# Newton's rounds of 26 small reciprocal square roots moved from VectorE to GpSimd in a 1-core transformer kernel

## The chip, the core and the metric

The kernel runs on one core of a Trainium2 chip. The core has a TensorE (PE in the profile; its weight loads are shown apart as PEld), a VectorE (DVE), a ScalarE (ACT), a GpSimd (POOL), and a SyncE (SP) that issues most of the transfers. Each engine works through its own queue in order; semaphores tie the engines together. The metric is device time in microseconds, the median of several executions. Inputs and outputs are float32.

## What is computed

Two transformer blocks on 256 tokens of width 1024. The first has two attentions side by side (a: global with grouped keys, b: a mixture of dilated windows), each with 8 heads of 64, whose q and k are normed per head and whose outputs are normed over all 512 columns:

```python
qa = apply_axial_rope(rms_norm(qa, qa_norm_g), tables)
ka = apply_axial_rope(rms_norm(ka, ka_norm_g), tables)
out_a = global_gqa_attention(qa, ka, va)
out_b = dilated_mixture_attention(rms_norm(qb, qb_norm_g), rms_norm(kb, kb_norm_g), vb)
mixed = jnp.concatenate([rms_norm(out_a, outa_norm_g), rms_norm(out_b, outb_norm_g)], axis=-1)
x = x + mixed @ w_out
x = x + conv_ffn(rms_norm(x, norm2_g), w_up, conv_w, conv_b, w_down)
```

The second block has two layers, each on 256 latent and 256 context tokens: a differential attention of 8 heads, a Mamba-2 scan beside it, and an MLP. Each head's output is normed per token:

```python
a = p[:, 0] - lam * p[:, 1]
o = jnp.einsum('bhqk,bkhe->bqhe', a, v)
...
(rmsnorm(o, subln_g) * (1.0 - lam_init))
```

In layer 1, the last, only the latent tokens' queries are computed (`lat_only`).

## The kernel before

Matrix products run on TensorE as three fp32r products (high by high, low by high, high by low). ScalarE casts a weight's high part (`whi`, `whB`), VectorE computes the low part (`wlo` at L137, `wlB` at L211), a 128x1024 subtraction each. Weights stream in while products run.

A norm needs 1/sqrt(v), which `rsqrt` (L213) computes without a table: L218 shifts the bits of v, L220 subtracts them from a magic number, and three rounds of Newton's method follow, L223 to L225, in place on two small tiles `nwt` and `nwy`. All of it is on VectorE, 128 partitions by 2, 4 or 8 columns. `rsqrt` is called 26 times:

- In the first block 10 times: `rt` for the tokens' norm (its consumers are ScalarE's `vA`, `vB`), the kv tile and six q and k tiles in `hstat` (consumers L569, L539, L542, L544; behind them ptq, the transposes on TensorE), and once for each half of the output in `weigh` (`mra`, `mrb`): L642 scales `oa` or `ob`, and ptm transposes it for the output product.
- In each attention of the second block 8 times, once per head, in `headnorm`: L1205 and L1206 prepare v, `rsqrt` follows, L1209 writes the normed head `o` from the accumulator `po`, and in the next step `headout` has TensorE transpose it (pto; two or four 128x128).

The attention of the second block is a software pipeline over units of a head: scores of unit i (pss on TensorE, maxima L1163 and L1164 on VectorE, exponentials `pr` on ScalarE), the transposes ptp of unit i−1, the weighing po of unit i−2, and the head's norm when its last unit is weighed. Between these steps a background stream puts products of the following heads' q, k and v (psq, psk, psv), of gates (psgs) and, at the end, of the scan (psB, psC, psxs) on TensorE. While `self.pin` is set, the order of TensorE's instructions stays nearly as the program writes it; the order on the other engines is the scheduler's, which places each instruction by its own estimates. `dk` (L1032) is a tile of the scan's decays that VectorE writes within head 1 of layer 0, from TensorE's ptcs and psdec. GpSimd has little to do: some memsets at the start, seven sums of squares (L444), the zeroing of halves of `klo` (L1099) for each head, and sums of squares in the scan (L1570, L1573).

Of the kernel before, what the change touches and what calls it, by code (L numbers as in the profile page):

```python
# [25 lines left out]
ADD, SUB, MUL, MIN, MAX = ALU.add, ALU.subtract, ALU.mult, ALU.min, ALU.max  # L26
# [78 lines left out]
class Build:  # L105
# [107 lines left out]
    def rsqrt(self, v, pool, n, tag="nw"):  # L213
        nc = self.nc
        p = v.shape[0]
        ti = pool.tile([p, n], F32, tag=tag + "t", name="nwt")
        y = pool.tile([p, n], F32, tag=tag + "y", name="nwy")
        nc.vector.tensor_scalar(out=ti.bitcast(I32), in0=v.bitcast(I32), scalar1=1, scalar2=None,  # L218
                                op0=ALU.arith_shift_right)
        nc.vector.tensor_scalar(out=y.bitcast(I32), in0=ti.bitcast(I32), scalar1=-1.0,  # L220
                                scalar2=float(0x5F3759DF), op0=MUL, op1=ADD)
        for _ in range(3):
            nc.vector.tensor_tensor(out=ti, in0=y, in1=y, op=MUL)  # L223
            nc.vector.scalar_tensor_tensor(out=ti, in0=ti, scalar=-0.5, in1=v, op0=MUL, op1=MUL)
            nc.vector.scalar_tensor_tensor(out=y, in0=ti, scalar=1.5, in1=y, op0=ADD, op1=MUL)  # L225
        return y

    def fnorm(self, src, kts, n, dim, pool):
# [1794 lines left out]
```

## Time and profile before

| | |
|---|---|
| Time, median of 3 runs | 2373.35 us (2372.89 to 2373.66) |
| The profiled execution | 2373.57 us |
| Its span, first to last instruction | 2371.8 us |
| Mean granted clock of TensorE | 0.996 |
| Busy: PE / PEld / DVE / ACT / POOL | 98% / 86% / 73% / 57% / 2% |
| GpSimd | 57.7 us in 68 instructions |

Busy time is the union of an engine's spans; a matmul's end is modelled, so a busy TensorE may still wait within a span. An instruction of VectorE, ScalarE or GpSimd lengthens the kernel only where TensorE, or the chain that ends last, waits for it.

### The profile page before, as it was taken

Reading aid. Unit: us, or ns where it says so; the run is one execution under the profiler, and the core shown is the slowest. Engines: PE = TensorE matmul, PEld = TensorE weight load, DVE = VectorE, ACT = ScalarE, POOL = GpSimd, SP = SyncE. Lnnn points to the kernel's source line nnn. Section 1 sums busy time; section 2 is a strip of 40 time slices with the busy share of each in tenths; the row PEclk is TensorE's granted clock in tenths of the full one; section 3 lists DMA queues with packets and bytes.
Section 4 is the critical chain, followed back from the end, with each engine's and each line's share of the span. In section 5 each row is a group of like instructions: output and inputs, shape, how many; then the busy total and the mean of one; then the engine's idle time right before and its main releaser. Section 6 shows DMA issues by size and latency. Waiting matters only on the chain.

```text
span 2371.8 us, 39549 instructions
## 1 busy us (share of the span) xinstructions
PE 2317.3 (98%) x15566; PEld 2036.8 (86%) x15566; DVE 1738.7 (73%) x3466; ACT 1345.2 (57%) x2681; POOL 57.7 (2%) x68
## 2 busy tenths in 40 slices
PE   8999999999999999999999999999999999999998
PEld 7889998888887887778897877899898888899998
DVE  6678866777687878996474334388788999976776
ACT  5566546667565666764243233247776676655553
POOL 1000000000000000100000000000000000000000
PEclk9999999999999999999999999999999999999999
DMA  7557674112433343336343453353224444365553
GB/s 273 172 190 263 227 256 147 57 71 67 112 116 128 114 138 120 114 124 229 110 140 145 153 220 126 123 189 121 92 94 143 156 134 161 115 214 179 189 184 107
DMA packets 75034, 356.59 MB, mean 150 GB/s; under 512 B 9184, under 2 KB 16352, under 8 KB 38368
## 3 DMA queue, kind: packets, MB, share of 16 engines
q1 hardware_dynamic: 71088, 349.31, 42.5%
q10 hardware_dynamic: 3760, 4.75, 0.6%
q8 instruction: 122, 2.00, 0.3%
q14 instruction: 64, 0.52, 0.1%
HBM read 340.15 MB, written 13.89 MB: 149 GB/s over the span
## 4 chain that ended last, share of the span: by engine, by line
PE 84%; DVE 8%; ACT 6%; issue 1%; DMA 1%; POOL 0%; SPq 0%; DVEq 0%; ACTq 0%; POOLq 0%
PE psm L331 22%; PE psxs L331 6%; PE psso L331 6%; PE psu L331 5%; PE psz L331 4%; PE psk L331 3%; PE psao L331 3%; PE psga L331 3%; PE psd L331 3%; PE psB L331 3%; PE psgs L331 2%; PE pso L331 2%; PE psv L331 2%; PE psy L331 2%; PE psC L331 2%; PE po L331 2%
## 5 line engine op out<-in xcount | busy, mean ns | idle before, releaser
L136 ACT CAST whi<-raw 128x1024 fp32r<-128x1024 f32 (+1 forms) x430 | 445.2, 1043 | 530.6 <-PE psm L331 262.0
L137 DVE TENSOR_TENSOR wlo<-raw,whi 128x1024 fp32r<-128x1024 f32 (+1 forms) x430 | 521.8, 1218 | 213.6 <-ACT whi L136 209.1
L331 PE MATMUL psm<-dh,whi 128*128 128x256 f32 (+1 forms) x576 | 182.7, 317 | 0.5 <-DVE x L1784 0.5
L331 PE MATMUL psm<-dl,whi 128*128 128x256 f32 (+1 forms) x576 | 182.4, 317 | 0.0
L331 PE MATMUL psm<-dh,wlo 128*128 128x256 f32 (+1 forms) x576 | 182.3, 317 | 0.0
L331 PE MATMUL psm<-hhi,whi 128*128 128x258 f32 (+2 forms) x544 | 179.5, 330 | 1.7 <-ACT whi L136 1.2
L331 PE MATMUL psm<-hlo,whi 128*128 128x258 f32 (+2 forms) x544 | 179.1, 329 | 0.4 <-DVE hlo L920 0.3
L331 PE MATMUL psm<-hhi,wlo 128*128 128x258 f32 (+2 forms) x544 | 177.8, 327 | 0.5 <-DVE wlo L137 0.5
L1485 ACT ACTIVATE E<-R,cstok 128x128 f32<-128x128 f32 x384 | 120.0, 390 | 37.4 <-PE psy L331 28.3
L331 PEld LDWEIGHTS psm<-dh,whi 128*128 128x128 f32 x576 | 108.6, 189 | 9.3 <-issue 1.9
L331 PEld LDWEIGHTS psm<-hhi,whi 128*128 128x128 f32 x544 | 103.1, 190 | 15.1 <-issue 2.9
L331 PEld LDWEIGHTS psm<-dh,wlo 128*128 128x128 f32 x576 | 108.7, 189 | 7.5
L331 PEld LDWEIGHTS psm<-dl,whi 128*128 128x128 f32 x576 | 108.5, 188 | 7.4
L331 PE MATMUL psxs<-hhi,whi 128*128 128x512 f32 x256 | 113.0, 442 | 0.0
L1784 DVE SCALAR_TENSOR_TENSOR x<-psm,mod,x 128x256 f32<-128x256 f32 x96 | 44.1, 482 | 93.1 <-PE psm L331 93.1
L331 PEld LDWEIGHTS psm<-hlo,whi 128*128 128x128 f32 x544 | 103.2, 190 | 9.3 <-DVE hlo L920 1.2
L331 PEld LDWEIGHTS psm<-hhi,wlo 128*128 128x128 f32 x544 | 103.2, 190 | 9.2 <-DVE wlo L137 0.7
L331 PE MATMUL psxs<-hlo,whi 128*128 128x512 f32 x256 | 100.3, 392 | 0.0
L331 PE MATMUL psxs<-hhi,wlo 128*128 128x512 f32 x256 | 100.2, 392 | 0.0
L1346 DVE SCALAR_TENSOR_TENSOR xT<-psxs,halfw,xT 128x510 f32<-128x510 f32 (+1 forms) x128 | 94.6, 743 | 0.5 <-ACT xT L1342 0.2
L1166 ACT ACTIVATE pr<-pss,mx 128x512 f32<-128x512 f32 (+1 forms) x96 | 58.4, 614 | 61.4 <-DVE mx L1164 60.3
L331 PE MATMUL psu<-hhi,whi 128*128 128x256 f32 x320 | 91.6, 286 | 0.5 <-ACT hhi L800 0.5
(487 smaller groups left out, 7002.6 us busy)
## 6 DMA issues: line engine op xcount, KB each, us to landing
raw<-in_w_m SPq DMA_DIRECT2D x68, 1024.0 KB, 4.9
araw<-in_ada SPq DMA_DIRECT2D x48, 1024.0 KB, 5.2
R<-csd SPq DMA_DIRECT2D x48, 512.0 KB, 6.2
raw<-in_w_up SPq DMA_DIRECT2D x22, 1024.0 KB, 4.9
raw<-in_w_qk SPq DMA_DIRECT2D x16, 1024.0 KB, 4.9
raw<-in_w_bc SPq DMA_DIRECT2D x16, 1024.0 KB, 5.0
raw<-in_w_xs SPq DMA_DIRECT2D x16, 1024.0 KB, 4.9
raw<-in_w_z SPq DMA_DIRECT2D x16, 1024.0 KB, 5.0
```

The source lines that it names most:

```text
L136: nc.scalar.copy(h, r)
L137: nc.vector.tensor_tensor(out=lo[:, :nk, :n], in0=r, in1=h.bitcast(F32), op=SUB)
L331: i = self.nc.tensor.matmul(*args, **kw)
L1166: nc.scalar.activation(out=pt_[:, i * kw:(i + 1) * kw], in_=ps[:, i * kw:(i + 1) * kw], func=AF.Exp, scale=0.125, bias=mx[:, i:i + 1], acc ...
L1346: nc.vector.scalar_tensor_tensor(out=y[:, :, lo:hi], in0=u[:, :, lo + o:hi + o], scalar=wj(j), in1=y[:, :, lo:hi], op0=MUL, op1=ADD)
L1485: nc.scalar.activation(out=E[:, d, h, :], in_=R[:, d, h, :], func=AF.Relu, scale=-1.0, bias=self.cs_tok[:, c, i:i + 1])
L1784: nc.vector.scalar_tensor_tensor(out=xs[col][:, k, :], in0=ps[:, t], scalar=self.mod[l][:, 40 + k, col:col + 1], in1=xs[col][:, k, :], op0 ...
```

## The change

The two integer steps of `rsqrt` stay on VectorE. Each round of Newton's method becomes four GpSimd instructions in place of three on VectorE: VectorE's fused form (multiply by a scalar, then by a tensor) is taken apart. All 26 calls change; the rounds' arithmetic is the same but for the order of roundings. Behind L222 the line numbers of the changed kernel are two higher.

```diff
--- before.py
+++ after.py
@@ -219,10 +219,12 @@
                                 op0=ALU.arith_shift_right)
         nc.vector.tensor_scalar(out=y.bitcast(I32), in0=ti.bitcast(I32), scalar1=-1.0,
                                 scalar2=float(0x5F3759DF), op0=MUL, op1=ADD)
+
         for _ in range(3):
-            nc.vector.tensor_tensor(out=ti, in0=y, in1=y, op=MUL)
-            nc.vector.scalar_tensor_tensor(out=ti, in0=ti, scalar=-0.5, in1=v, op0=MUL, op1=MUL)
-            nc.vector.scalar_tensor_tensor(out=y, in0=ti, scalar=1.5, in1=y, op0=ADD, op1=MUL)
+            nc.gpsimd.tensor_tensor(out=ti, in0=y, in1=y, op=MUL)
+            nc.gpsimd.tensor_tensor(out=ti, in0=ti, in1=v, op=MUL)
+            nc.gpsimd.tensor_scalar(out=ti, in0=ti, scalar1=-0.5, scalar2=1.5, op0=MUL, op1=ADD)
+            nc.gpsimd.tensor_tensor(out=y, in0=ti, in1=y, op=MUL)
         return y
 
     def fnorm(self, src, kts, n, dim, pool):
```

GpSimd's queue now holds the rounds in the order of the calls, with the memsets between them. Before, the queue holds nothing of them; the rows below stand at head 0 of layer 0 (ss is v, nwt and nwy the two small tiles).

```order
L1101 MEMSET klo 64x512 x6
L224 TENSOR_TENSOR nwt<-nwy 128x4
L225 TENSOR_TENSOR nwt<-nwt,ss 128x4
L226 TENSOR_SCALAR nwt<-nwt 128x4
L227 TENSOR_TENSOR nwy<-nwt,nwy 128x4
L224 TENSOR_TENSOR nwt<-nwy 128x4
```

Two more rounds and two memsets of klo follow, and then head 1's rounds; a round waits for the one before it, and the first for VectorE's L220.

On VectorE at the same place, before (rt, rot and qhl belong to the q product of a later head, mx to the maxima of a next unit, o to this head):

```order
L220 TENSOR_SCALAR nwy<-nwt 128x4
L1070 TENSOR_TENSOR rot<-rot,cons 128x256
L223 TENSOR_TENSOR nwt<-nwy 128x4
L1111 TENSOR_TENSOR qhl<-psq_5160,qhl 64x256
L224 SCALAR_TENSOR_TENSOR nwt<-nwt,ss 128x4
L1071 TENSOR_TENSOR rot<-rt,rot 128x256
...
L1163 TENSOR_REDUCE mx_5311<-pss_5309 128x2
L224 SCALAR_TENSOR_TENSOR nwt<-nwt,ss 128x4
L1164 TENSOR_SCALAR mx_5300<-mx_5300 128x2
L1164 TENSOR_SCALAR mx_5311<-mx_5311 128x2
L225 SCALAR_TENSOR_TENSOR nwy<-nwt,nwy 128x4
L1209 TENSOR_TENSOR o_5238<-po_4806,nwy 128x512
```

And now:

```order
L220 TENSOR_SCALAR nwy<-nwt 128x4
L1072 TENSOR_TENSOR rot<-rot,cons 128x256
L1113 TENSOR_TENSOR qhl<-psq_5190,qhl 64x256
L1073 TENSOR_TENSOR rot<-rt,rot 128x256
L1113 TENSOR_TENSOR qhl<-psq_5190,qhl 64x256
L1211 TENSOR_TENSOR o_5271<-po_4836,nwy 128x512
L1113 TENSOR_TENSOR qhl<-rot,qhl 64x256 x2
L1165 TENSOR_REDUCE mx_5333<-pss_5331 128x2
L1165 TENSOR_REDUCE mx_5344<-pss_5342 128x2
```

Before, the nine instructions of the rounds took turns with ten others; now L1211 (L1209 of before) stands five rows behind L220, and two of the qhl rows and the maxima have moved behind it. At the other heads L1211 stands right behind L220, or with one wlo, wlB or maximum between.

On TensorE, most rows are where they were; at the last two heads of each layer pto has moved. At head 6 of layer 0, before (psB are products of the scan in the background, pto the transposes of the head's o, ptp those of a unit's probabilities):

```order
L331 MATMUL psB<-hhi,wlo 128x512
L331 MATMUL psB<-hhi,whi 128x512
L331 MATMUL psB<-hlo,whi 128x512
L331 MATMUL psB<-hhi,wlo 128x512
L331 MATMUL psB<-hhi,whi 128x512
L326 MATMUL pto_7122<-cons,o_7063 128x128 x4
L331 MATMUL po_6933<-V,pT_7079 128x128 x4
L326 MATMUL ptp_7135<-cons,pr_7006 128x128 x4
L331 MATMUL psB<-hlo,whi 128x512
```

And now:

```order
L333 MATMUL psgs<-hhi,wlo 128x512
L333 MATMUL psB<-hhi,whi 128x512
L333 MATMUL psB<-hlo,whi 128x512
L328 MATMUL pto_7173<-cons,o_7114 128x128 x4
L333 MATMUL po_6981<-V,pT_7130 128x128 x4
L328 MATMUL ptp_7186<-cons,pr_7054 128x128 x4
L333 MATMUL psB<-hhi,wlo 128x512
L333 MATMUL psB<-hhi,whi 128x512
L333 MATMUL psB<-hlo,whi 128x512
```

Of the seven psB matmuls that stood between the gate's and pto, two still do, and five come behind ptp. At head 7 of layer 0 pto has moved ahead by one matmul, at head 6 of layer 1 by four.

## Rows read from the trace of the kernel before

**Rows 1.** The page: span, and part 1, busy time (share) xinstructions.

```profile
span 2371.8 us, 39549 instructions
...
PE 2317.3 (98%) x15566; PEld 2036.8 (86%) x15566; DVE 1738.7 (73%) x3466; ACT 1345.2 (57%) x2681; POOL 57.7 (2%) x68
```

**Rows 2.** TensorE's waits: who for whom, us in total, times, longest.

```profile
PE pto L326 <- DVE o L1209: 9.4, 5, 3.4
...
PE pto L326 <- DVE dk L1032: 2.2, 1, 2.2
PE ptm L326 <- DVE oa L642: 2.0, 2, 1.7
```

**Rows 3.** Timeline of TensorE: start, us, instruction, [idle time before, releaser].

```profile
448.40 0.66 PE L326 MATMUL pto<-cons,o 128*128 128x128 f32 x4 [3.44 <-DVE o L1209]
...
535.82 0.60 PE L326 MATMUL pto<-cons,o 128*128 128x128 f32 x4
...
613.58 0.39 PE L331 MATMUL psB<-hhi,wlo 128*128 128x512 f32 x1
613.81 0.39 PE L331 MATMUL psB<-hhi,whi 128*128 128x512 f32 x1
614.10 0.66 PE L326 MATMUL pto<-cons,o 128*128 128x128 f32 x4
...
627.73 0.66 PE L326 MATMUL pto<-cons,o 128*128 128x128 f32 x4 [0.27 <-DVE o L1209]
...
1672.73 0.69 PE L326 MATMUL pto<-cons,o 128*128 128x128 f32 x2 [3.19 <-DVE o L1209]
...
1801.76 0.41 PE L326 MATMUL pto<-cons,o 128*128 128x128 f32 x2 [0.34 <-DVE o L1209]
```

**Rows 4.** Stretches: busy us of each engine, granted clock (PEclk), DMA, GB/s.

```profile
core 0: us, PE busy (x) PEld busy (x) DVE busy (x) ACT busy (x) POOL busy (x), PEclk, DMA share, GB/s
449.80:453.30 3.50, 3.50 (x11) 2.73 (x10) 3.46 (x8) 2.79 (x5) 0.00 (x0) 0.51 0.00 0
478.80:485.00 6.20, 3.97 (x27) 3.46 (x26) 4.46 (x14) 2.90 (x10) 0.00 (x0) 1.00 0.00 0
1671.80:1678.60 6.80, 5.87 (x28) 5.87 (x29) 5.21 (x16) 6.02 (x16) 0.00 (x0) 0.50 0.44 153
```

**Rows 5.** Tile nwt: xcount, ns min/median/max, first and last start, shapes.

```profile
L223 DVE TENSOR_TENSOR nwt<-nwy x78: 152/161/171, 20.5 to 1800.6; 128x2 f32<-128x2 f32 x33, 128x4 f32<-128x4 f32 x27, 128x8 f32<-128x8 f32 x18
```

**Rows 6.** Timeline of VectorE.

```profile
16.01 1.36 DVE L211 TENSOR_TENSOR wlB<-raw,whB 128x1024 fp32r<-128x1024 f32 x1 [1.14 <-ACT whB L210]
...
442.38 0.16 DVE L220 TENSOR_SCALAR nwy<-nwt 128x4 int32<-128x4 int32 x1
...
447.65 0.69 DVE L1209 TENSOR_TENSOR o<-po,nwy 128x512 f32<-128x512 f32 x1
...
533.72 0.69 DVE L1209 TENSOR_TENSOR o<-po,nwy 128x512 f32<-128x512 f32 x1
...
610.41 0.17 DVE L220 TENSOR_SCALAR nwy<-nwt 128x4 int32<-128x4 int32 x1
...
1667.28 0.17 DVE L220 TENSOR_SCALAR nwy<-nwt 128x2 int32<-128x2 int32 x1
...
1799.22 0.17 DVE L220 TENSOR_SCALAR nwy<-nwt 128x2 int32<-128x2 int32 x1
...
1801.18 0.42 DVE L1209 TENSOR_TENSOR o<-po,nwy 128x256 f32<-128x256 f32 x1
```

**Rows 7.** Timeline of GpSimd.

```profile
0.24 0.10 POOL L2014 MEMSET const-float32-0.0<- 128x1 f32 x1 [0.24 <-issue]
...
16.43 2.32 POOL L444 TENSOR_TENSOR sqa<-sqa,sq 128x256 f32<-128x256 f32 x2 [0.15 <-ACT sq L443]
```

**Rows 8.** Tile sqa on GpSimd: xcount, ns min/median/max.

```profile
L444 POOL TENSOR_TENSOR sqa<-sqa,sq x7: 724/742/1520, 12.2 to 18.0; 128x256 f32<-128x256 f32 x7
```

**Rows 9.** Tile ssq on GpSimd.

```profile
L1573 POOL TENSOR_TENSOR ssq<-ssq,u x19: 1288/1615/1934, 710.0 to 2089.1; 128x512 f32<-128x512 f32 x19
```

## The prediction, before the changed kernel was run

> **What bounds the kernel now.** I first read the busy shares: TensorE (PE) is at 98% and VectorE (DVE) at 73%, while GpSimd (POOL) works 57.7 us of 2371.8 [rows 1]. So a VectorE instruction costs time only where TensorE stands waiting for it. Next comes the table of TensorE's waits. Its longest entry is the one that this change touches: pto, the transposes of a head's normed output o, waited 9.4 us for o in five places. ptm, the transposes of the first block's output, waited 2.0 us for oa, and one pto waited 2.2 us for dk [rows 2]. The table has six waits of pto in all, for sixteen heads, so at ten heads TensorE arrived no earlier than its data. Where it did wait, the rows give the price: 3.44 us at the first head of layer 0, 3.19 us at the first of layer 1, 0.27 and 0.34 us at the last head of each layer [rows 3]; at ptm it was 1.7 [rows 2].
>
> After the two long gaps the granted clock is 0.51 in 449.80 to 453.30 and 0.50 in 1671.80 to 1678.60, the lower of TensorE's two levels (1.2 GHz, not 2.4) [rows 4]. TensorE was busy for 3.50 and 5.87 us there; at the full clock this would be half, so these stretches cost about 1.7 and 2.9 us on top of the gaps.
>
> **What the change takes from VectorE.** A call of rsqrt loses nine VectorE instructions; 26 calls lose 234, at 161 ns each 37.7 us of busy time [rows 5]. I cost this gain at nothing by itself, since VectorE is not the bound. It counts in the chain from L220 to the consumer: in the last head of layer 1, where nothing is interleaved, L220 starts at 1799.22 and takes 0.17, and L1209 starts at 1801.18. That is 1.79 us for nine instructions [rows 6].
>
> **What it adds on GpSimd.** Twelve instructions in a row, each needing the one before. The trace has no GpSimd arithmetic on 2 to 8 columns, so I bound it. Below: the smallest GpSimd instruction is a 128x1 memset of 0.10 us [rows 7]. Above: the 128x256 TENSOR_TENSOR, 0.74 us at the median and 0.72 at the least [rows 8]. The 128x512 one takes 1.29 at the least [rows 9], so 256 columns more cost 0.56 us, 2.2 ns each, and the line through both has about 0.16 us left at no columns. Between dependent instructions there is a gap: the pair at 16.43 took 2.32 us, and 1.52 (the longest) and 0.72 of it are work, so 0.08 is gap [rows 7, 8]. I take 0.16 + 0.08 = 0.24 us for one, an estimate, since 2 to 8 columns are nearest to the line's end at none; 12 of them are 2.88 us. A handover to GpSimd showed 0.15 us of idle time after ScalarE's release [rows 7]; with two of about 0.14, to and from VectorE, the chain is 3.16 us in place of 1.79. **An exposed call loses 1.4 us.** At the lower bound (0.18 per instruction, 2.44 in all) it loses 0.65; at the upper bound (0.82, 10.1 in all) 8.3. With 0.35 it loses 2.7.
>
> **The order changes too.** VectorE's remaining instructions used to be slipped between the rounds; now L1209 stands almost directly behind L220, and the max reductions come after it. Of the first heads this matters most.
> - Layer 0, head 0: L220 starts at 442.38 and L1209 at 447.65, 5.3 us for a chain that needs 1.8 by itself, because ten others stand between [rows 6]. Then L220 ends at 442.54, L1209 could start at 445.70, take 0.69, and pto follow 0.06 later, at 446.45 in place of 448.40 [rows 3]: **−1.9**.
> - Layer 1, head 0: L220 ends at 1667.45 [rows 6], so by the same sum pto could run at 1671.1 in place of 1672.73, −1.6. But one 1.22 us wlB stands between. The row of L211 that met GpSimd's 128x256 took 1.36 us while that one took 1.52 in place of 0.74 [rows 6 to 8]: the two hold each other up. With wlB's whole length added the gain is −0.4. I take **−1.0**.
>
> The page "SBUF — State Buffer" of the Trainium skill, section "SBUF: two separate sides", states that a VectorE instruction with two SBUF inputs and a GpSimd one that reads SBUF take the shared port pair by an exclusive lock, for the whole instruction. The row of 1.52 us agrees; by it the gain at layer 1's head 0 would be −0.4 and not −1.6.
>
> **Where it costs.** Exposed fully: the norm of the a half in the first block (L642, then ptm, where TensorE waits already) and the same of the b half, **+1.4** each. The last heads of both layers, with waits already: layer 0 +1.4, and +0.2 because pto stands one matmul earlier (psB matmuls start 0.23 apart [rows 3]): **+1.6**; layer 1 **+1.3**. Layer 0, head 6: L220 ends at 610.58 [rows 6], L1209 would start at 613.74, end at 614.43, and pto go at 614.5. TensorE reached it at 614.10 with seven psB matmuls ahead; five of them now stand behind pto, so it arrives at 612.96: **+1.5**. Layer 1's head 6 is the same with four matmuls: **+1.2**. Head 1 of layer 0: dk stands behind L1209 on VectorE, which comes 0.75 later: **+0.75**. Head 5, with a wlo between: **+0.4**. The first block's q and k tiles have their transposes well behind, except kb's second: **+0.4**; rt, on which vA waits and behind it ScalarE's casts, with the kv tile **+0.5**.
>
> **What hides the rest.** Head 3 of layer 0: L1209 ends at 534.41 and pto starts at 535.82 [rows 3, 6], 1.4 us, which the longer chain just uses up. Head 4 is alike; heads 1 to 5 of layer 1 have more: 0. If a GpSimd instruction costs 0.35, heads 3 and 4 cost 1.3 each as well. The klo memsets share the queue, but each stands behind the rounds it follows, and the klo products come microseconds later: 0.
>
> **The sum.** First block 1.4 + 1.4 + 0.4 + 0.5 = 3.7; layer 0 −1.9 + 0.75 + 0.4 + 1.5 + 1.6 = 2.35; layer 1 −1.0 + 1.2 + 1.3 = 1.5; together +7.5. The clock: the gap at layer 0's head 0 shrinks from 3.44 to 1.5 us and I expect its slow stretch to go, −1.7. Around the wait for dk, a gap of 2.2 us, the clock stays at 1.00 [rows 2, 4], so layer 1's may go as well, −2.9 at even odds, −1.5; ptm's gap grows from 1.7 to 3.1 and may bring one, +1.7. Net −1.5. The profiled execution took 2373.57 us (span 2371.8, and 1.8 around it), 0.2 above the median; 2373.57 + 7.5 − 1.5 = 2379.6, against the median 2379.4. I forecast **2379 us**, +0.24%. A measurement of this kernel can tell about 0.2% (4.7 us) from no change, so this is near the edge.
>
> **The rivals.**
> 1. *Faster.* The place is the first head of each layer. If both slow stretches go and no wlB holds GpSimd up there, these two heads return 1.9 + 1.6 + 1.7 + 2.9 = 8.1 us. With the lower bound per instruction the ten costs above, 10.4 us together, shrink by about 0.6 each to 4.4: net −3.7, 2370 us. It decides when an instruction costs under about 0.20 us with its gap; for it speaks that the idle times there are the longest of all, against it that no arithmetic row on GpSimd is near so short.
> 2. *Dearer instructions.* If one costs 0.35, or VectorE's long two-input instructions hold GpSimd up in most calls, each of the ten costs 1.3 more, the two gains shrink by as much and heads 3 and 4 of layer 0 join: 14 × 1.3 = 18 on top of 2379, 2397; at 0.30, half of that, 2388. For it: the 1.52 us row. Against it: in the exposed calls VectorE stands waiting. The page "GPSIMD Engine Reference" of the Trainium skill, section "Elementwise — side-by-side cycle accounting", gives a two-input add 1.96 times VectorE's time; by it an instruction would be an estimated 0.32 plus the gap, and the time near 2406. No run shows this at so few columns.
> 3. *Nothing to tell.* The gains at the heads 0 and the costs elsewhere cancel, 2371 to 2377: it needs the first two terms of the clock without the third, −4.6, on top of the sum of +7.5, or two of the exposed calls hidden after all, by an arrival of TensorE that I place too early.
>
> **How the numbers follow.** Forecast (2375 to 2384) 0.42, dearer 0.18, nothing to tell 0.25, faster 0.15. Of the forecast's part some 0.12 lies below 2378.1, where +0.2% begins, so: slower 0.48, same 0.37, faster 0.15. The range reaches from the faster case, 2369, to the middle of the dearer one, 2393, with about one in ten left outside at either end; the forecast's own is 2375 to 2384.
>
> **What would show it.** In the changed profile: GpSimd has 312 instructions more, of 0.15 to 0.2 us, starting 0.24 apart; L220's end to L1209's start about 3.2 us at the last heads; pto's wait at layer 0's head 0 near 1.5 us, without a slow stretch; ptm's first wait about 3 us; new waits of 1.2 to 1.9 us at heads 6 and 7 of both layers; dk's wait near 3. What would prove me wrong: GpSimd instructions of half a microsecond or under 0.2 apart, TensorE gaps that do not move with L1209, or slow stretches in places where none was.

## The result, and the profile after

| | before | changed |
|---|---|---|
| Time, median of 4 runs | 2373.12 us (2372.00 to 2373.66) | 2406.45 us (2402.03 to 2407.95) |
| Ratio, 95% interval | | 1.0133 [1.0122, 1.0145] |
| Profiled execution, span | 2373.57, 2371.8 us | 2407.61, 2405.8 us |
| TensorE busy, idle within the span | 2317.3, 54.5 us | 2326.2, 79.6 us |
| TensorE below full clock, sum of all stretches (5.7 and 4.8 us of it behind TensorE's last instruction) | 22.8 us | 42.3 us |

The change loses 33.3 us, 1.3%, well beyond the forecast of +0.24% and above the range. The page of the changed kernel has the span and the busy shares, to be read against [rows 1]:

```profile
span 2405.8 us, 39641 instructions
...
PE 2326.2 (97%) x15566; PEld 2042.4 (85%) x15566; DVE 1706.0 (71%) x3232; ACT 1347.7 (56%) x2681; POOL 130.2 (5%) x380
```

VectorE gave up 32.7 us of busy time and GpSimd took on 72.5. TensorE, which does the same 15566 products, is busy for 8.9 us more and idle for 25.1 more; together that is the 34.0 by which the span grew. So there are two losses to find: waits, and a lower clock. The table of TensorE's waits (who for whom; us in total, times, longest) answers [rows 2]:

```profile
PE pto L328 <- DVE o L1211: 20.5, 12, 2.8
...
PE pto L328 <- DVE dk L1034: 6.8, 2, 3.6
PE ptm L328 <- DVE oa L644: 4.6, 2, 4.4
...
PE po L333 <- ACT pT L613: 2.6, 2, 2.2
```

The waits of pto for o went from 9.4 us in 5 places to 20.5 in 12, those for dk from 2.2 in one to 6.8 in two, ptm's for oa from 2.0 to 4.6, and po's wait for pT in the first block is new in its length. TensorE's timeline shows where they lie (start, us, instruction, idle time before and its releaser; compare [rows 3]):

```profile
104.88 0.47 PE L328 MATMUL ptm<-cons,oa 128*128 128x128 f32 x1 [4.38 <-DVE oa L644]
...
462.53 0.66 PE L328 MATMUL pto<-cons,o 128*128 128x128 f32 x4 [1.92 <-DVE o L1211]
...
495.64 1.12 PE L328 MATMUL pto<-cons,o 128*128 128x128 f32 x4 [3.15 <-DVE dk L1034]
...
526.06 1.12 PE L328 MATMUL pto<-cons,o 128*128 128x128 f32 x4 [2.77 <-DVE o L1211]
...
653.19 0.66 PE L328 MATMUL pto<-cons,o 128*128 128x128 f32 x4 [2.22 <-DVE o L1211]
...
1697.85 0.44 PE L328 MATMUL pto<-cons,o 128*128 128x128 f32 x2 [2.52 <-DVE o L1211]
...
1719.64 0.44 PE L328 MATMUL pto<-cons,o 128*128 128x128 f32 x2 [1.55 <-DVE o L1211]
...
1746.01 0.69 PE L328 MATMUL pto<-cons,o 128*128 128x128 f32 x2 [3.63 <-DVE dk L1034]
...
1810.19 0.44 PE L328 MATMUL pto<-cons,o 128*128 128x128 f32 x2 [1.54 <-DVE o L1211]
...
1837.87 0.41 PE L328 MATMUL pto<-cons,o 128*128 128x128 f32 x2 [2.21 <-DVE o L1211]
```

104.88 is the first block's a half. 462.53, 495.64, 526.06 and 653.19 are heads 0, 1, 2 and 7 of layer 0; 1697.85, 1719.64, 1746.01, 1810.19 and 1837.87 are heads 0, 1, 2, 5 and 7 of layer 1, where dk is written within head 2. The waits at the two heads 0 shrank, from 3.44 to 1.92 and from 3.19 to 2.52, and every other one of these rows grew or is new.

GpSimd's instructions, by the tile nwt (ns min/median/max, which answers [rows 5]) and in the timeline of the last head of layer 1:

```profile
L224 POOL TENSOR_TENSOR nwt<-nwy x78: 193/198/1110, 20.5 to 1836.2; 128x2 f32<-128x2 f32 x33, 128x4 f32<-128x4 f32 x27, 128x8 f32<-128x8 f32 x18
...
1834.03 0.19 POOL L224 TENSOR_TENSOR nwt<-nwy 128x2 f32<-128x2 f32 x1 [6.59 <-DVE nwy L220]
1834.30 0.20 POOL L225 TENSOR_TENSOR nwt<-nwt,ss 128x2 f32<-128x2 f32 x1
```

One takes 0.19 to 0.20 us, and they start 0.27 to 0.28 apart. The median hides 13 of the 312: eleven took 1.04 to 1.26 us and two about 0.53, together some 11 us more than undisturbed. Eight of the 13 lie in the first block and five at heads (2 and 5 of layer 0; 0, 5 and 6 of layer 1). VectorE's timeline shows what happened around the chain (compare [rows 6]):

```profile
520.63 0.17 DVE L220 TENSOR_SCALAR nwy<-nwt 128x4 int32<-128x4 int32 x1
521.48 1.23 DVE L211 TENSOR_TENSOR wlB<-raw,whB 128x1024 fp32r<-128x1024 f32 x1 [0.68 <-ACT whB L210]
525.31 0.69 DVE L1211 TENSOR_TENSOR o<-po,nwy 128x512 f32<-128x512 f32 x1 [2.61 <-POOL nwy L227]
...
1743.22 0.42 DVE L1211 TENSOR_TENSOR o<-po,nwy 128x256 f32<-128x256 f32 x1 [3.42 <-POOL nwy L227]
...
1745.54 0.42 DVE L1034 TENSOR_TENSOR dk<-psdec,cstok 128x256 f32<-128x256 f32 x1
...
1833.71 0.17 DVE L220 TENSOR_SCALAR nwy<-nwt 128x2 int32<-128x2 int32 x1
1837.30 0.42 DVE L1211 TENSOR_TENSOR o<-po,nwy 128x256 f32<-128x256 f32 x1 [3.42 <-POOL nwy L227]
```

At the last head L220 ends at 1833.88 and L1211 starts at 1837.30: 3.42 us, where it was 1.79 [rows 6]. At head 2 of layer 0 it is 520.80 to 525.31, 4.51 us, because one GpSimd instruction there lasted 1.25 us, beside a wlB that started 0.03 ahead of it:

```profile
521.51 1.25 POOL L226 TENSOR_SCALAR nwt<-nwt 128x4 f32<-128x4 f32 x1
```

wlB itself took 1.23, no longer than the 1.22 named in the prediction: GpSimd waited and VectorE did not. At head 2 of layer 1 VectorE stood still for 3.42 us in front of L1211 (1743.22), and dk, the seventh instruction behind it in the queue, came at 1745.54 and held TensorE until 1746.01. In the table of what VectorE's L1211 waited for, the row on GpSimd is the sum of such stops (us, times):

```profile
  POOL nwy L227: 48.0, 16
```

That is 3.0 us at each of the sixteen heads. Last, the clock, by stretches (columns as in [rows 4]):

```profile
58.13:64.96 6.83, 6.83 (x34) 5.63 (x33) 2.37 (x6) 4.24 (x9) 2.40 (x12) 0.50 0.68 251
102.50:109.33 6.83, 4.26 (x17) 3.78 (x18) 2.80 (x4) 1.18 (x2) 1.13 (x6) 0.50 0.12 38
146.88:153.71 6.83, 6.42 (x26) 5.61 (x27) 5.57 (x11) 1.17 (x2) 0.00 (x0) 0.50 0.00 0
495.03:498.44 3.41, 2.80 (x13) 2.80 (x14) 2.42 (x9) 2.45 (x9) 0.00 (x0) 0.50 0.01 2
525.75:529.16 3.41, 3.10 (x14) 3.01 (x15) 2.88 (x7) 1.79 (x6) 0.63 (x2) 0.50 0.00 0
1744.31:1751.14 6.83, 5.13 (x24) 5.14 (x25) 6.08 (x19) 5.06 (x13) 0.00 (x0) 0.50 0.01 4
```

The first three stretches lie in the first block: behind po's wait of 2.2 us, around ptm's wait of 4.38, and at ptm's wait for the b half. Before, TensorE kept the full clock from 23 us to 449. It was busy there for 6.83 + 4.26 + 6.42 = 17.5 us, half of which, 8.8 us, the full clock would have saved. The lower clock is not that of one execution alone: the mean granted clock is 0.992 to 0.994 in the four executions of the changed kernel, and 0.994 to 0.998 in thirteen of the kernel before.

### The profile page after: what moved, and what is told of

The parts are those of the page before. It is cut to its first block, busy times and chain, and to the rows that moved or that the text cites. A ratio compares the mean times of both kernels' runs of the same rounds, so it can differ in the third digit from the quotient of the medians.

```text
span 2405.8 us, 39641 instructions
## 1 busy us (share of the span) xinstructions
PE 2326.2 (97%) x15566; PEld 2042.4 (85%) x15566; DVE 1706.0 (71%) x3232; ACT 1347.7 (56%) x2681; POOL 130.2 (5%) x380
## 3 DMA queue, kind: packets, MB, share of 16 engines
q1 hardware_dynamic: 71088, 349.31, 42.3%
## 4 chain that ended last, share of the span: by engine, by line
PE 75%; DVE 11%; ACT 8%; POOL 3%; issue 2%; DMA 1%; DVEq 0%; POOLq 0%; ACTq 0%
PE psm L333 22%; PE psxs L333 6%; PE psso L333 5%; PE psu L333 5%; PE psz L333 4%; PE psd L333 3%; PE psao L333 3%; PE pso L333 2%; PE psB L333 2%; PE psy L333 2%; PE psga L333 2%; PE psk L333 2%; PE psgs L333 2%; PE psv L333 2%; PE psC L333 2%
## 5 line engine op out<-in xcount | busy, mean ns | idle before, releaser
L1348 DVE SCALAR_TENSOR_TENSOR xT<-psxs,halfw,xT 128x508 f32<-128x508 f32 (+1 forms) x128 | 95.3, 747 | 0.8 <-ACT xT L1344 0.4
```

Source lines behind the costliest of these rows:

```text
L1348: nc.vector.scalar_tensor_tensor(out=y[:, :, lo:hi], in0=u[:, :, lo + o:hi + o], scalar=wj(j), in1=y[:, :, lo:hi], op0=MUL, op1=ADD)
```

## The experiments

Four theories were set against each other. *Length*: what costs is the time from L220 to the consumer, whichever engine spends it. *Blocking*: VectorE stands still in front of L1211, and all that is queued behind comes late. *Port*: VectorE's long instructions hold GpSimd's up. *Clock*: the loss is mostly slow stretches. In all kernels of the transformer below `rsqrt` has an argument that says for each call where the rounds run; but for what a diff shows, all other code is the same. "Mean chain" is the time from L220's end to the start of the multiplication by its result, as a mean over the sixteen heads, worked out from VectorE's timeline: 2.62 us before, 3.73 changed. "Shortest chain" is the least of the sixteen, where nothing is interleaved and nothing holds it up: 1.80 us before, 3.41 changed.

**Where it is lost: first block against heads.** The rounds run on GpSimd only in the first block's ten calls, or only in the sixteen heads (the diff shows the first).

```diff
-    def rsqrt(self, v, pool, n, tag="nw"):
+    def rsqrt(self, v, pool, n, tag="nw", eng=True):
...
-                rs = self.rsqrt(ss[:, :nu], wk, nu)
+                rs = self.rsqrt(ss[:, :nu], wk, nu, eng=False)
```

> The rounds on GpSimd in the first block's ten calls alone; the heads' sixteen calls have them on VectorE as before. In the changed kernel TensorE's instructions stand 15.5 us later at the end of the first block, 25.4 at the end of layer 0's heads and 37 at the end of layer 1's, 34 at the end. If the loss is made by each call at its own place, this kernel is 15 to 16 us slower than before (2388 to 2390). If what the first block loses is given back later, or heads lose more because the first block comes late, it is below 2380.

> The rounds on GpSimd in the second block's sixteen heads alone. If places add up, 33 less the first block's 15 to 16: 17 to 19 us slower than before, 2390 to 2392, with the same waits of TensorE at the heads as in the changed kernel. If they don't add, the two kernels together differ from 33 by more than 3 us.

The first block alone: 2387.16 us, ratio 1.0058 [1.0043, 1.0073], +13.2, a little less than expected. The heads alone: 2393.57, ratio 1.0083 [1.0068, 1.0098], +19.6, a little more. The sum, 32.8, is the change's 33.3: the two parts add up, and neither is small. The clock's part lies in the first block: that kernel is below full clock for 36.4 us (mean granted clock 0.991 to 0.994 in its four executions), the heads' kernel for 21.9 (0.995 to 0.996), no more than before. The heads' loss is waits: TensorE is idle for 17.8 us more and busy for 2.6.

**VectorE's stop taken away.** On top of the heads-only kernel, the multiplication by the norm moves out of `headnorm` and is issued behind the next scores' maxima, so that these no longer stand behind it.

```diff
+                return po, rs
+
+            def headout(h, pr):
+                po, rs = pr
...
+                with ExitStack() as late:
+                    if "mx" in head:
+                        late.enter_context(self.tc.issue_after(head.pop("mx")))
+                    nc.vector.tensor_tensor(out=o2[:, :nu, :], in0=po[:, :nu * 128].rearrange("p (u e) -> p u e", u=nu),
+                                            in1=blast(rs, 128), op=MUL)
...
```

> As the kernel with the rounds on GpSimd in the heads alone, but the multiplication that makes a head's o is put on VectorE behind the maxima of the next scores, where it stood before the change, in place of right behind the second integer step. Theory 'blocking': the loss comes from VectorE, whose queue stands up to 3.4 us behind the waiting multiplication; with the maxima ahead of it VectorE's stalls fall from 3.4 to some 2 us a head and half or more of the 17 to 19 us goes: 2378 to 2384. Theory 'length': the chain from the second integer step to the multiplication is 3.5 us in place of 1.8, and o comes when the chain ends; the order doesn't matter and the time is 2389 to 2392. In heads 0 both give TensorE's wait near 3 us again.

2397.13 us, ratio 1.0099 [1.0082, 1.0116], no better than the 2393.57 of the heads alone. In the view of that multiplication's line (what it waited for, and who waited for it; us, times):

```profile
  POOL nwy L228: 14.5, 8
...
  PE pto L334: 26.4, 10
```

VectorE's wait for GpSimd fell from 48.1 us at sixteen heads to 14.5 at eight, and with it TensorE's wait for dk, which only stands behind the multiplication, from 6.7 us in two places to 2.0 in one. But TensorE's wait for o rose from 20.4 to 26.4, because the edit itself makes o later: the mean chain is 5.16 us in place of 3.73. So the stop has a price of its own, 4.7 us at dk, and more was lost at o than was freed. Neither theory's time came, and an edit that changes both cannot tell how much of the 19.6 us is blocking.

**The heads 0 alone.** GpSimd only at head 0 of each layer, where the prediction saw a gain.

```diff
-                rs = self.rsqrt(ss[:, :nu], wk, nu)
+                rs = self.rsqrt(ss[:, :nu], wk, nu, eng=h == 0)
```

> The rounds on GpSimd in the first head of each layer alone, the two places that gained in the changed kernel: layer 0's head 0 took 1.5 us off TensorE's wait and the stretch at half clock behind it went, 2.9 us together; layer 1's took 0.7 off and its stretch at half clock went, 2.6 together. If that gain stands by itself: 4 to 6 us faster than before, 2367 to 2370. If VectorE, held up there, gives it back at the following heads, or the clock falls somewhere else instead: 2371 to 2375, no difference that can be told.

2373.45 us, ratio 0.9999 [0.9990, 1.0008]: nothing. The gaps did shrink, to 1.92 us at 448.15 and 2.43 at 1674.36, and the slow stretch at layer 1's head 0 went. But TensorE has a new wait at head 2 of layer 1, whose rounds are on VectorE as before:

```profile
1719.20 0.44 PE L334 MATMUL pto<-cons,o 128*128 128x128 f32 x2 [1.98 <-DVE dk L1040]
```

And layer 0 has two stretches of half clock in place of one (columns as in [rows 4]):

```profile
448.14:451.55 3.41, 3.40 (x14) 3.29 (x15) 2.26 (x6) 1.12 (x5) 0.38 (x1) 0.50 0.00 0
509.58:512.99 3.41, 3.41 (x16) 3.12 (x14) 2.47 (x6) 2.31 (x9) 0.00 (x0) 0.50 0.40 101
```

A third, early in the first block, which this edit does not touch, lasted 6.83 us in place of 3.41. So part of the scatter of the clock is not the edit's. The branch of the expectation that came true is the second: the smaller gaps gave 2.3 us, and 2.0 of it is handed back at head 2.

**The heads that the prediction costed at nothing.** GpSimd only at heads 3 and 4 of layer 0 and heads 1 to 4 of layer 1.

```diff
-                rs = self.rsqrt(ss[:, :nu], wk, nu)
+                rs = self.rsqrt(ss[:, :nu], wk, nu, eng=(h in (3, 4) if nu == 4 else h in (1, 2, 3, 4)))
```

> The rounds on GpSimd only in six heads that the prediction costed at nothing: heads 3 and 4 of layer 0 and 1 to 4 of layer 1; all else as before. In the changed kernel TensorE lost 1 us at the two of layer 0 and, with a stretch at half clock, 7.6 at heads 1 and 2 of layer 1. Theory 'own': these heads lose it by their own longer chain, and it is lost here too: 7 to 9 us slower than before, 2381 to 2383. Theory 'carried over': they lost it because VectorE came to them late, held up at head 0 of layer 1, which here has its rounds on VectorE: within 2 us of before.

2381.60 us against 2375.64, ratio 1.0027 [1.0016, 1.0038], +6.0. The time is the one that theory "own" gave, and not within 2 us of before. The kernel is that of before up to head 3 of layer 0, so what is lost there and at head 4 is not carried over from earlier calls. TensorE's timeline has new waits at and behind the six heads:

```profile
565.05 0.66 PE L334 MATMUL pto<-cons,o 128*128 128x128 f32 x4 [0.63 <-DVE o L1217]
...
1722.96 0.44 PE L334 MATMUL pto<-cons,o 128*128 128x128 f32 x2 [1.78 <-DVE dk L1040]
...
1773.98 0.39 PE L339 MATMUL psga<-hhi,wlo 128*128 128x256 f32 x1 [1.30 <-DVE wlo L137]
...
1785.17 0.44 PE L334 MATMUL pto<-cons,o 128*128 128x128 f32 x2 [0.30 <-DVE o L1217]
```

At head 1 of layer 1, where TensorE waits for 1.55 us in the changed kernel, it does not wait here. The start of the multiplication on VectorE and of pto on TensorE at this head, before, with the heads 0 alone, and here:

```profile
1690.71 0.42 DVE L1209 TENSOR_TENSOR o<-po,nwy 128x256 f32<-128x256 f32 x1
1695.40 0.38 PE L326 MATMUL pto<-cons,o 128*128 128x128 f32 x2
...
1694.01 0.42 DVE L1217 TENSOR_TENSOR o<-po,nwy 128x256 f32<-128x256 f32 x1
1694.49 0.44 PE L334 MATMUL pto<-cons,o 128*128 128x128 f32 x2
...
1696.17 0.43 DVE L1217 TENSOR_TENSOR o<-po,nwy 128x256 f32<-128x256 f32 x1 [3.40 <-POOL nwy L228]
1698.52 0.38 PE L334 MATMUL pto<-cons,o 128*128 128x128 f32 x2
```

Before, o is ready 4.27 us ahead of TensorE. With the heads 0 alone on GpSimd it is 0.06 us ahead, although this head's own chain is 1.8 us as before. Here, with the longer chain of 3.40 us at this head but not at head 0, it is 1.92 ahead; in the changed kernel, which has both, it is 1.49 late. Head 0 takes more of this cover than head 1's own chain does. Counted from head 0's pto (1672.73 before, 1674.36 with the heads 0 alone), TensorE comes to head 1 after 20.13 us in place of 22.67, as the slow stretch behind head 0 went, and VectorE starts the multiplication after 19.65 in place of 17.98. At head 2 the wait for dk is 1.78 us here, 1.98 with the heads 0 alone and 3.63 in the changed kernel. So the time alone misleads, and both theories have a part: the two heads of layer 0 lose by their own chains, and of what heads 1 and 2 of layer 1 lose in the changed kernel, these rows put half or more down to head 0.

**Instructions by themselves.** A program of its own in place of the transformer: chains of six rounds on GpSimd (three for 128x256), alone and beside back-to-back instructions of VectorE.

```diff
+            section("dve", 4, nc.vector, 6, None, 0)
+            section("two", 2, nc.gpsimd, 6, None, 0)
+            section("four", 4, nc.gpsimd, 6, None, 0)
+            section("eight", 8, nc.gpsimd, 6, None, 0)
+            section("wide", 256, nc.gpsimd, 3, None, 0)
+            section("ctwo", 4, nc.gpsimd, 6, two_in, 8)
+            section("cone", 4, nc.gpsimd, 6, one_in, 8)
+            section("cmix", 4, nc.gpsimd, 6, mixed_in, 12)
+            section("cred", 4, nc.gpsimd, 6, reduce_in, 12)
```

> A program of its own that computes nothing of the reference: the same chain of multiplications, six rounds each, first on VectorE, then on GpSimd with nothing beside it at 2, 4, 8 and 256 columns, then at 4 columns on GpSimd while VectorE runs, back to back, 128x1024 subtractions of two SBUF tiles, 128x1024 multiplications of one SBUF tile, 128x512 products of a PSUM and an SBUF tile, and maxima over a 128x512 PSUM tile. Expected from the changed kernel's trace: 0.28 us from one GpSimd instruction's start to the next with nothing beside it, 0.20 on VectorE. Theory 'port': beside the two-tile subtractions each GpSimd instruction waits for one of them to end, 1.0 us and more apiece, and beside the other three kinds it is as fast as alone. Theory 'any neighbour': all four kinds slow it, in proportion to the bytes they move.

VectorE's chain took 0.162 us for an instruction. GpSimd's groups (total us, mean ns) and two places of its timeline, beside VectorE's two-input (ctwo) and one-input (cone) instructions:

```profile
L1886 POOL TENSOR_TENSOR ttwo<-ttwo,vtwo 128x2 f32<-128x2 f32 x6 | 1.2, 196 | 0.5
...
52.82 1.18 POOL L1888 TENSOR_TENSOR yctwo<-tctwo,yctwo 128x4 f32<-128x4 f32 x1
54.08 0.20 POOL L1885 TENSOR_TENSOR tctwo<-yctwo 128x4 f32<-128x4 f32 x1
...
64.53 0.65 POOL L1888 TENSOR_TENSOR ycone<-tcone,ycone 128x4 f32<-128x4 f32 x1
65.25 0.20 POOL L1885 TENSOR_TENSOR tcone<-ycone 128x4 f32<-128x4 f32 x1
```

Alone, an instruction took 0.195 to 0.20 us, at 2 columns as at 8. Beside VectorE's 128x1024 with two SBUF inputs each one took 1.18 until these were done, beside the one with a single SBUF input 0.65, and beside a product with an input from PSUM or a maximum over PSUM 0.20. VectorE's two-input instruction took 1.224 us, as in the transformer, where the median is 1.22; for the 0.693 us of the other no run has the same instruction without a neighbour. The port theory is right about the two-input instructions and wrong in that only they hold GpSimd up; each hold-up is as long as the VectorE instruction that it meets. That any neighbour slows GpSimd is ruled out by the two kinds that read PSUM.

**Fewer rounds on GpSimd.** The changed kernel with one and with two rounds in all calls (the diff shows the first).

```diff
-        for _ in range(3):
...
+            for _ in range(1):
```

> The changed kernel with two of the three rounds left out in all 26 calls (the norms are then coarse): four GpSimd instructions in place of twelve, a chain of 1.3 us from the second integer step to the consumer, where before the change it was 1.8 and with it 3.5. Theory 'length': the loss goes with the chain, 33 us for 1.7 us more; at 1.3 us there is none, and the first heads gain a little: 2366 to 2373. Theory 'order': what costs is that VectorE's other work moved behind the consumer; it is so here too, and 5 us or more stay: 2378 or more.

> As the last, with one of three rounds left out: a chain of 2.4 us. Theory 'length', if a line: (2.4 - 1.8) / 1.7 of 33, 11 us slower than before, 2384. If slack hides the first part of it, as it does where TensorE arrives after the data, less than a third: under 2381; the last round then costs more than the second.

One round: 2362.95 us, ratio 0.9949 [0.9932, 0.9965], mean chain 1.34, shortest 1.21. Two: 2376.10, ratio 1.0009 [1.0000, 1.0018], mean chain 2.56, shortest 2.32. With three it is 2406.45 at 3.73 and 3.41. VectorE's multiplication stands as close behind L220 with one round as with three, so the theory that the new order costs is out, and the time is even below the 2366 to 2373 of *length*. The second round costs 13 us and the third 30: the price climbs as the cover runs out.

**The length on VectorE.** Six rounds on VectorE in all calls, and no instruction on GpSimd.

```diff
-        for _ in range(3):
...
+            for _ in range(6):
```

> The kernel before with six rounds on VectorE in place of three, in all 26 calls: the chain is 3.6 us as on GpSimd, with no handover and no other engine's hold-up, and VectorE has 37.7 us more to do. Theory 'length': about as slow as the changed kernel, 2400 to 2412. Theory 'GpSimd' (handover and hold-up are what costs): less than half of it, 2380 to 2390.

2416.66 us, ratio 1.0174 [1.0159, 1.0189], above the 2400 to 2412 of *length*; shortest chain 3.56 as expected, mean chain 5.21, because other work of VectorE stands between the rounds. A loss larger than the change's comes with no GpSimd, no handover and no port in it. TensorE is idle for 81.6 us, 27.1 more than before and nearly the 25.1 of the changed kernel; the rest is the clock, with 64.0 us below full speed and 17.3 us more of busy time. VectorE does not stand still in front of the multiplication here, but it is at work on the rounds, and what is queued behind comes late in either case.

**A shorter chain.** Two rounds on VectorE, with other constants, which give 1/sqrt within 5e-7.

```diff
-                                scalar2=float(0x5F3759DF), op0=MUL, op1=ADD)
-        for _ in range(3):
-            nc.vector.tensor_tensor(out=ti, in0=y, in1=y, op=MUL)
-            nc.vector.scalar_tensor_tensor(out=ti, in0=ti, scalar=-0.5, in1=v, op0=MUL, op1=MUL)
-            nc.vector.scalar_tensor_tensor(out=y, in0=ti, scalar=1.5, in1=y, op0=ADD, op1=MUL)
+                                scalar2=float(0x5F1FFFF9), op0=MUL, op1=ADD)
...
+            for c, b in ((-0.703952253, 1.6819141), (-0.5, 1.5000004)):
+                nc.vector.tensor_tensor(out=ti, in0=y, in1=y, op=MUL)
+                nc.vector.scalar_tensor_tensor(out=ti, in0=ti, scalar=c, in1=v, op0=MUL, op1=MUL)
+                nc.vector.scalar_tensor_tensor(out=y, in0=ti, scalar=b, in1=y, op0=ADD, op1=MUL)
```

> The rounds on VectorE as before, but two in place of three in all 26 calls, with another magic number and other constants in the first of them, so that two rounds end within 5e-7 of 1/sqrt (three of the old ones within 1.6e-7). The chain from the second integer step to the consumer falls from 1.8 to 1.2 us with no handover. Theory 'length': one round of four GpSimd instructions on GpSimd, 1.3 us, gave 2363; this is shorter: 2358 to 2364, faster than both kernels. If that gain came from VectorE's order or from its 234 instructions less, little of it shows: 2369 to 2374.

2362.87 us, ratio 0.9946 [0.9930, 0.9963]: faster than both kernels. Mean chain 1.74, shortest 1.21. VectorE has only 78 instructions fewer here, so the gain of one round on GpSimd, which is the same, needs no saving of 234. From its page, and from the table of TensorE's waits:

```profile
span 2361.2 us, 39474 instructions
...
PE 2312.5 (98%) x15566; PEld 2032.6 (86%) x15566; DVE 1729.7 (73%) x3388; ACT 1345.8 (57%) x2681; POOL 57.5 (2%) x68
...
PE pto L334 <- DVE o L1217: 4.9, 4, 2.3
```

TensorE is idle for 48.7 us where it was 54.5, and busy for 4.8 less; the waits of pto for o halved [rows 1, 2]. No stretch below full clock is left in either layer's heads, and all such stretches come to 12.8 us in place of 22.8.

## Why the prediction was wrong

TensorE's starts, changed minus before, give what each stage cost: +15.5 us at the end of the first block, 10.0 more over layer 0's heads, 11.7 more over layer 1's, and 3.1 given back behind them. Expected were 3.7, 2.35 and 1.5, and −1.5 for the clock.

| term | expected | measured, TensorE's wait after minus before |
|---|---|---|
| ptm, a half | +1.4 | +2.7 (1.68 to 4.38) |
| ptm, b half | +1.4 | +1.5 (in total 0.3 to 1.8) |
| q, k and kv tiles | +0.9 | about +4: po for pT 2.2, psqk for wlB and whB 1.0 and 1.1 (not the change's, see below), ptq for hy 1.1, less 1.3 at another ptq |
| layer 0: heads 0, 1 | −1.9, +0.75 | −1.5, +0.9, and 1.1 more at ptcs |
| layer 0: head 2 | not priced | +0.6 (2.14 to 2.77) |
| layer 0: heads 3, 4, 5 | 0, 0, +0.4 | +0.2, +0.6, +1.0 |
| layer 0: heads 6, 7 | +1.5, +1.6 | +1.7, +1.95 |
| layer 1: head 0 | −1.0 | −0.7 |
| layer 1: heads 1, 2, 5 | 0, 0, 0 | +1.55, +3.63, +1.54 |
| layer 1: heads 6, 7 | +1.2, +1.3 | +2.25, +1.9 |
| clock | −1.5 | +8.9 (TensorE's busy time) |

The measured waits add up to the 25 us by which TensorE is idle longer. The two of psqk do not recur in the kernel that has the first block alone on GpSimd, and a wait of 1.17 us of psqk for wlB stands in the kernel with the heads alone, whose first block is as before; so about 2 us of the first block's 15.5 lie between executions, and the +13.2 of the first of these kernels is the better figure.

**What held.** The heads 0 gain, by nearly what was said; dk in layer 0 waits 3.15 us where about 3 was named; the last heads cost what was said to within half a microsecond in layer 0. The size of a GpSimd instruction alone was right too, 0.195 us where "0.15 to 0.2" stood, but its gap was 0.08 and the start-to-start time 0.275, not 0.24, so that the undisturbed chain took 3.42 us and not 3.16. In the wording of the prediction that is an "instruction" of 0.275, on the way to the second rival's 0.30.

**The clock, the largest single miss.** The prediction let a slow stretch go in layer 0, half of one in layer 1, and brought one of 1.7 us in at ptm. The two at the heads 0 went, as expected; but others came at heads 1 and 2 of layer 0 and head 2 of layer 1, and three of 6.83 us in the first block, where 8.8 us were lost; slow stretches where none was stood among its own signs of being wrong. So the first block's +15.5 is about half clock and half waits. What failed is the rule by which it placed stretches, from one execution: a long gap brings one, and a gap of 2.2 us does not. Here a stretch stands behind a gap of 2.18 us, and in the experiment on the heads 0 behind one of 1.92. The kernel with six heads on GpSimd runs the same instructions as the kernel before up to head 3 of layer 0, with the same gaps, 3.44 us at head 0 and 2.21 at head 1, and there it is the other way round (columns as in [rows 4]):

```profile
449.80:453.30 3.50, 3.50 (x23) 3.06 (x24) 2.39 (x7) 3.50 (x11) 0.00 (x0) 1.00 0.00 0
482.23:485.64 3.41, 3.41 (x11) 2.63 (x10) 1.47 (x4) 0.04 (x1) 0.00 (x0) 0.50 0.00 0
```

Full clock behind the gap of 3.44, half clock behind that of 2.21. That layer 0's stretch at head 0 went is thus in part luck: it can be missing with the rounds on VectorE too.

**"What hides the rest", the step that failed in the waits.** The prediction set the slack of a head in the trace of before against the growth of the same head's own chain, and found that heads 1 to 5 of layer 1 cost 0. They have between 1.49 and 4.27 us of slack before, and yet they cost 6.7 us: heads 1 and 5 by o itself, and head 2 by dk, which was not waited for there before and now stands behind a VectorE that is still for 3.4 us. Two things were left out. First, slack is not a head's own: a longer chain and a lost slow stretch at head 0 took 4.2 of the 4.27 us at head 1 with its own chain unchanged, and gave TensorE a wait of 1.98 us for dk at head 2. The a half of the first block shows the same: its own chain grew by 1.55 us (1.80 to 3.35), its wait by 2.7, as VectorE came to it late from the call before. Second, only the consumer o was followed. An in-order engine that waits delays all that is queued behind it, and wlB, wlo and dk have consumers on TensorE too. Layer 0's head 2 was overlooked: of the 9.4 us in [rows 2], the rows at [rows 3] make up 7.24, and the 2.16 left are a fifth exposed place.

**The hold-ups.** The prediction had the mechanism from the 1.52 us row and priced it once, at head 0 of layer 1. It happened to 13 instructions, for 0.3 to 1.1 us each. At the five heads a wlB or wlo stands between L220 and L1211 on VectorE; the eight of the first block were held up beside wlB or beside a multiplication of hy. If all of it reached TensorE undiminished, this would be an estimated 11 us, 4.6 of them at the heads against their 19.6; so it is not the larger part, its effect on the clock aside. The page "SBUF — State Buffer" of the Trainium skill, section "SBUF: two separate sides", describes an exclusive lock on a port pair that the two engines share, taken by a VectorE instruction with two SBUF inputs or in a 2-port mode; the row of 1.25 us and the chains beside two-input instructions agree with it. That a one-input 128x1024 multiplication holds GpSimd up too, for 0.65 us, is measured here; no run shows in which mode it runs.

**The rivals.** "Dearer instructions" was the nearest, 2388 to 2397, and it named both of its causes; what kept it at 18 in a hundred was the remark that "in the exposed calls VectorE stands waiting", and at heads with a wlB or wlo in between VectorE did not only wait. The page "GPSIMD Engine Reference", section "Elementwise — side-by-side cycle accounting", of the Trainium skill gave a factor of 1.96 and with it 2406, which is the time measured, but by chance: on 2 to 8 columns the factor is 0.195 to 0.161, 1.21, and 1.40 from one start to the next (0.275 to 0.196).

**What the experiments settle.** The waits go with the length of the chain, whichever engine spends it. By the shortest chain, TensorE's idle time is 47.5 us with one round on GpSimd (1.21), 48.7 with two on VectorE (1.21), 54.5 before (1.80), 57.8 with two rounds on GpSimd (2.32), 79.6 in the changed kernel (3.41) and 81.6 with six on VectorE (3.56); the times are 2363, 2363, 2373, 2376, 2406 and 2417. It rises by some 10 us from 1.21 to 2.32, and by 22 from there to 3.41. The mean chain tells less: from 3.73 to 5.21 the time rises by only 10 us, most of it clock.

Not settled is how the loss divides between an o that comes late and a queue that comes late behind it. By the table of waits, 15.2 of the 25.1 us are for o, oa and ob and 4.6 for dk, but the late place of o at one head can itself come from the head before, and six rounds on VectorE make both late as well. The hold-ups' part has no more than the estimate above: no kernel here ran the rounds on GpSimd with no such neighbour. Open is also what decides where a slow stretch falls. The clock's part varies from one execution to the next: the kernel with GpSimd in the first block alone had stretches of 6.83, 3.41 and 3.41 us there, not three of 6.83 and one of 3.41.

## What to carry to other kernels

Moving small dependent instructions from a busy engine to an idle one is paid in latency: count the chain from its first input to its last consumer, handovers and gaps between dependent instructions included, before counting the busy time that is freed. Cover seen in the old trace is cover for the old queue: a head that gains at one place brings TensorE earlier to the next, and its cover shrinks there. Follow every instruction that stands behind the new wait on its engine to its own consumer. Where a chain sits between an engine that never rests and its next operand, look first for fewer steps in the chain: doing with two rounds on VectorE was worth 12.8 us here, where moving three cost 33.

## What the runs showed of the hardware

- A GpSimd TENSOR_TENSOR or TENSOR_SCALAR on 128 partitions took 0.195 to 0.20 us at 2, 4 and 8 columns alike, and a dependent one started 0.275 to 0.28 us behind it; VectorE's took 0.16, 0.196 apart.
- GpSimd was held up for the length of one VectorE instruction, 1.18 us beside 1.224 and 0.65 beside 0.693, and this for each of its instructions as long as VectorE had more of that kind in a row. VectorE's two-input instruction lost nothing to these short neighbours; beside a 128x256 of GpSimd it had taken 1.36 us [rows 6]. VectorE instructions that read PSUM did not hold GpSimd up.
- TensorE spent 19.5 us more below full clock than before, and was busy there for 32.0 us in place of 16.1, which at half speed makes 7.9 of the 8.9 us by which it was busy longer. Added waits did not always bring it: at the heads alone, 17.8 us more of idle time came with no more time below full clock (21.9 us, and 22.8 before).
- The same instructions with the same gaps had half clock behind a gap of 3.44 us and full clock behind one of 2.23 in one execution, and the reverse in another kernel that is the same up to there.
